# Three 256-column products per row tile in place of one of 512 and one of 256, with the operand rows packed in halves

## The chip, the cores and the metric

The kernel runs on one core of one Trainium2 chip. The core has five engines that work side by side: TensorE (PE in the profile; its weight loads are listed apart as PEld), VectorE (DVE), ScalarE (ACT), GpSimd (POOL) and SyncE (SP, which here issues DMAs). A product on TensorE has a stationary side of 128x128 numbers, loaded before it, and a moving side of up to 512 columns that is read from SBUF and added into a PSUM bank of 512 float32 columns. The metric is the time of one execution on the device in microseconds; 1596.77 us before the change (median of three runs, 1596.67 to 1596.89).

## What is computed

One decoder layer over 256 tokens and 16 meta tokens, model width 2048, all in float32:

```python
def hybrid_mixer(xn, w_in, ...):
    proj = xn @ w_in                       # 2048 x 13336
    ...                                    # forgetting attention (8 heads), gated linear attention (4 heads)
    y = sigmoid(gate_fox) * (o_fox @ w_o_fox) + sigmoid(gate_gla) * (o_gla @ w_o_gla)
    return y @ w_out

h = h + hybrid_mixer(rmsnorm(h, norm_mix_g), ...)
h = h + square(relu(rmsnorm(h, norm_mlp_g) @ w_ff1)) @ w_ff2     # 2048 -> 8192 -> 2048
return rmsnorm(h, final_norm_g)[:, 16:]
```

Nearly all of the work is in matrices times 256 or 272 tokens: `w_in`, `w_o_fox`, `w_o_gla`, `w_out`, `w_ff1`, `w_ff2`.

## The kernel before

Activations lie transposed, channels on the 128 partitions and tokens along the row. To reach float32 accuracy with TensorE's faster float32r type, both sides are cut in two: `hi` is the number rounded to float32r, `lo` is what is left. A product of two such numbers takes three partial products, hi by hi, hi by lo and lo by hi.

The weights come in blocks of 2048x128 (`w_all`, in the order of `stream()`), each as two halves of 8 row tiles. For each half SP loads `raw` (512 KB), ScalarE copies it to `whi` (line 120), VectorE subtracts to `wlo` (line 121). Five buffers of each kind go round.

One block is then multiplied by an *operand* of 16 row tiles (`of` has 8): `x` (the normalised input), `of` and `og` (the outputs of the two attentions), `y` (their gated sum), `x2` (the normalised residual) and `a` (the squared ReLU, one for each of four groups `g` of 2048 channels). The profile leaves numbers out of names, so its `x` stands for `x` and `x2`.

`gemm2` (line 139) does it: for each row tile `k`, `mac2` issues two products. Line 136 multiplies `whi` by 512 columns, the 256 columns of hi and the 256 of lo side by side, into a whole PSUM bank. Line 137 multiplies `wlo` by the 256 columns of hi into the bank's first half. The bank's halves must be added at the end: `total` (line 165) and `add_residual` (line 856) copy the second half to `evb` on ScalarE (lines 168 and 858) and add on VectorE (lines 171 and 860).

`operand` (line 218) lays a row tile out in 544 elements, of which 512 are used, from element 16: hi's 256 columns, then lo's 256. So each row tile starts 2176 bytes behind the one before.

`x` has a layout of its own (272 columns, with the meta tokens) and is used by `gemm_all` (lines 153 to 155, three products of 272 columns) and by `gemm2`. The first seven blocks have their own products (lines 345 and 350). In the last four blocks of `w_ff2` all `lo` products come first (line 912), and then the `hi` products by token halves (line 928), where one product reads 128 columns of hi and 128 columns of lo: two runs with 128 columns between them.

TensorE's order of products is that of the source, moved by a scheduler that interleaves the next block's first row tiles with the last ones of the block before where weights are ready early.

Of the kernel before, what the change touches and what calls it, by code (L numbers as in the profile page):

```python
# [7 lines left out]
F32 = mybir.dt.float32  # L8
F32R = mybir.dt.float32r
# [3 lines left out]
ALU = mybir.AluOpType  # L13
# [52 lines left out]
def trunk(ctx: ExitStack, tc: tile.TileContext, hT, w_small, w_all, consts, w_alpha2, out):  # L66
# [3 lines left out]
    def nm(s):  # L70
        serial[0] += 1
        return f"{s}_{serial[0]}"
# [11 lines left out]
    def bank(pool, s):  # L84
        return pool.tile([P, 512], F32, tag="bank", name=nm(s))
# [49 lines left out]
    def mac2(ps, hi, lo, x, first, last):  # L135
        nc.tensor.matmul(ps, hi, x, start=first, stop=False)  # L136
        nc.tensor.matmul(ps[:, 0:NT], lo, x[:, 0, :], start=False, stop=last)  # L137

    def gemm2(w, x, k0=0, nk=KT):

        ps = bank(pg, "ps")
        for k in range(nk):
            hi, lo = w(k0 + k)
            mac2(ps, hi, lo, x[:, k], k == 0, k == nk - 1)
        issued()
        return ps
# [18 lines left out]
    def total(ps, t=None):  # L165

        b = tmp.tile([P, NT], F32, tag="evb", name=nm("evb"))
        nc.scalar.copy(b, ps[:, NT:512])  # L168
        if t is None:
            t = tmp.tile([P, NT], F32, tag="evt", name=nm("evt"), bufs=4)  # L170
        nc.vector.tensor_tensor(t, ps[:, 0:NT], b, op=ALU.add)  # L171
        return t

    def split_to(dst_hi, dst_lo, src):
        nc.scalar.copy(dst_hi, src)
        nc.vector.tensor_tensor(dst_lo, src, dst_hi.bitcast(F32), op=ALU.subtract)
# [40 lines left out]

    def operand(pool, name, nk=KT, at=0, **kw):


        row = 2 * NT + 32
        t = pool.tile([P, at + nk * row], F32R, name=nm(name), **kw)
        t = t[:, at:].rearrange("p (k r) -> p k r", r=row)
        return t[:, :, 16 : 16 + 2 * NT].rearrange("p k (o t) -> p k o t", t=NT)


    h = keep.tile([P, KT, NA + 3], F32, name="h")
# [26 lines left out]
    def gain(i, k):  # L254
        return h[:, k, NA + i : NA + i + 1]
# [201 lines left out]

    def og_tile():
        if not og_box:
            og_box.append(operand(keep, "og", tag="s2"))  # L460
        return og_box[0]

    def gla_gates(ts):
# [30 lines left out]
    def gla_head(hd, sg, ready=None):  # L494
# [129 lines left out]
        def scale():  # L624
            for i in range(4):
                j = 4 * hd + i
                nc.vector.scalar_tensor_tensor(oT[:, i, :], oT[:, i, :], ggn[:, j : j + 1], rg, op0=ALU.mult,
                                               op1=ALU.mult)
                nc.vector.tensor_tensor(oT[:, i, :], oT[:, i, :], st["sg"][:, i, :], op=ALU.mult)
                split_to(og_tile()[:, j, 0, :], og_tile()[:, j, 1, :], oT[:, i, :])  # L630

        later(2, outputs)
        later(3, sums)
# [48 lines left out]
    cum.close()  # L682
    branches = ExitStack()
    late = branches.enter_context(tc.tile_pool(name="late", bufs=1, reuse_waits="tile"))
    of = operand(late, "of", FOX_H, 32)
    negc = late.tile([P, FOX_H, NA], F32, name="negc")
    nc.gpsimd.dma_start(negc.rearrange("p h t -> p (h t)"), fdram.to_broadcast([P, FOX_H * NA]))
    fox = ExitStack()
# [16 lines left out]
    def fox_head(hd):  # L705
# [71 lines left out]
        def out_v():  # L777
            po = bank(px, "pof")
            three(po[:, 0:NT], va, pa, True, False)
            nc.tensor.matmul(po[:, P:NT], vb, pT, start=False, stop=True)  # L780
            nc.scalar.copy(of[:, hd, 0, :], po[:, 0:NT])
            nc.vector.tensor_tensor(of[:, hd, 1, :], po[:, 0:NT], of[:, hd, 0, :].bitcast(F32),
                                    op=ALU.subtract)
            nc.scalar.copy(og4[:, four], corners(po[:, 0:NT]))

        def out_corners():
# [9 lines left out]
        def fill_corners(pu, vz, pz):  # L796
            nc.tensor.matmul(pu[:, 2 * P : 3 * P], vz, pz, start=True, stop=True)
            nc.vector.tensor_tensor(og4, og4, pu[:, 2 * P : 3 * P].rearrange("p (h c q) -> p h c q", c=2, q=NM),
                                    op=ALU.add)
            hi, lo = (of[:, hd - 3 : hd + 1, o, :].rearrange("p h (c q) -> p h c q", q=P)[:, :, :, P - NM :]  # L800
                      for o in range(2))
            split_to(hi, lo, og4)

        later(1, turn_v)
        later(2, turn_p)
# [20 lines left out]
    for j0 in range(0, KT, 2):  # L826
        gates = ahead if j0 == 0 else [gate() for _ in range(4)]
        w = next_weights()
        for j in range(2):
            t = total(gemm2(w, of, k0=8 * j, nk=8))  # L830
            nc.vector.tensor_tensor(gates[2 * j], gates[2 * j], t, op=ALU.mult)
        for j in range(2):
            t = total(gemm2(next_weights(), og))
            nc.vector.tensor_tensor(t, gates[2 * j + 1], t, op=ALU.mult)
            nc.vector.tensor_tensor(yf[:, j0 + j, :], gates[2 * j], t, op=ALU.add)
    y = operand(keep, "y", tag="s1")
    for j in range(KT):
        split_to(y[:, j, 0, :], y[:, j, 1, :], yf[:, j, :])
    mix.close()
    branches.close()  # L840
    gat = ctx.enter_context(tc.tile_pool(name="gat", bufs=2, reuse_waits="tile"))
# [1 line left out]


    ht = h[:, :, NM:NA]
    x2 = operand(keep, "x2", tag="s2")

    def square_sum(j, acc):
        if j == 0:
# [4 lines left out]
            nc.gpsimd.tensor_tensor(acc, acc, sq, op=ALU.add)  # L854

    def add_residual(j, ps):
        b = tmp.tile([P, NT], F32, tag="evb", name=nm("evb"))
        nc.scalar.copy(b, ps[:, NT:512])
        nc.vector.tensor_tensor(ht[:, j, :], ps[:, 0:NT], ht[:, j, :], op=ALU.add)
        nc.vector.tensor_tensor(ht[:, j, :], ht[:, j, :], b, op=ALU.add)  # L860

    acc2 = gat.tile([P, NT], F32, tag="acc", name="acc2", bufs=1)
    for j in range(KT):
        add_residual(j, gemm2(next_weights(), y))
        nc.scalar.activation(x2[:, j, 0, :], ht[:, j, :], AF.Identity, scale=gain(1, j))
        nc.vector.scalar_tensor_tensor(x2[:, j, 1, :], ht[:, j, :], gain(1, j),
                                       x2[:, j, 0, :].bitcast(F32), op0=ALU.mult, op1=ALU.subtract)
        square_sum(j, acc2)
    r2b = keep.tile([P, NT], F32, tag="rb", name="r2b")

# [4 lines left out]


    def relu2(a, f, ps):
        t = total(ps)
        nc.vector.scalar_tensor_tensor(t, t, 0.0, r2b, op0=ALU.max, op1=ALU.mult)
        s = gat.tile([P, NT], F32, tag="asq", name=nm("asq"))  # L880
        nc.vector.tensor_tensor(s, t, t, op=ALU.mult)
        split_to(a[:, f, 0, :], a[:, f, 1, :], s)

    acc = gat.tile([P, NT], F32, tag="acc", name="acc3", bufs=1)
    for g in range(NG):
        a = operand(keep, "a", tag="s1")
        held = []
        for f in range(KT):
            ps = gemm2(next_weights(), x2)
            if g == 0 and f == 0:  # L890
                held.append(ps)
                continue
            if g == 0 and f == 1:
                relu2(a, 0, held.pop())
            relu2(a, f, ps)
        last = g == NG - 1
        for j in range(KT - NL if last else KT):
            add_residual(j, gemm2(next_weights(), a))
            if last:
                square_sum(j, acc)  # L900
                nc.scalar.activation(ht[:, j, :], ht[:, j, :], AF.Identity, scale=gain(2, j))
                if j == 0:
                    tc.keep_in_program_order(nc.scalar.preload_act_table_set("natural_log_exp_and_others"))


    whi = keep.tile([P, NL, KT, P], F32R, tag="s2", name="whi_last")
    ends = []
    for n in range(NL):
        j, ps = KT - NL + n, bank(pg if n < 3 else px, "ps")
        w = next_weights(whi[:, n])  # L910
        for k in range(KT):
            nc.tensor.matmul(ps[:, 0:NT], w(k)[1], a[:, k, 0, :], start=(k == 0), stop=(k == KT - 1))  # L912
        nc.vector.tensor_tensor(ht[:, j, :], ps[:, 0:NT], ht[:, j, :], op=ALU.add)
        ends.append((j, w, ps))

    def half(t0, between, within=None):


        tok = slice(t0, t0 + P)
        sqs = []  # L920
        for n, (j, w, ps) in enumerate(ends):
            for k in range(KT):
                if within and n == NL - 1 and k == 4:
                    ahead = within()
                elif not (within and n == NL - 1 and k > 4):
                    ahead = None
                with tc.issue_after(ahead) if ahead else nullcontext():
                    nc.tensor.matmul(ps[:, NT:], w(k)[0], a[:, k, :, tok], start=(k == 0), stop=(k == KT - 1))  # L928
            between[n]()
            for t in (ps[:, NT : NT + P], ps[:, NT + P :]):  # L930
                nc.vector.tensor_tensor(ht[:, j, tok], t, ht[:, j, tok], op=ALU.add)
            sq = gat.tile([P, P], F32, tag="sq", name=nm("sq"), bufs=4)
            nc.scalar.activation(sq, ht[:, j, tok], AF.Square)
            nc.scalar.activation(ht[:, j, tok], ht[:, j, tok], AF.Identity, scale=gain(2, j))
            if n < NL - 2:
                nc.gpsimd.tensor_tensor(acc[:, tok], acc[:, tok], sq, op=ALU.add)
            else:
                sqs.append(sq)
        return sqs
# [119 lines left out]
```

## Time and profile before

| what | value |
|---|---|
| median of three runs | 1596.77 us |
| profiled execution, span | 1595.0 us |
| PE, 9812 products | busy 99% of the span |
| PEld, 9812 weight loads | 90% |
| VectorE | 66% |
| ScalarE | 50% |
| DMA engines, mean | about half busy, 184 GB/s |
| granted TensorE clock | 1.00 of full speed from 0 to 1400 us, 0.99 after |

How to read it: a product's duration in the profile is from its start to the end of its passage through the array, and products overlap. A product of 512 columns is listed with 393 ns and one of 256 columns with 281 ns, but the next one starts earlier than that. What a product costs when the array is never idle is the time from its start to the next start. The chain view gives that: its pieces are times between starts, and their sum is the span.

### The profile page before, as it was taken

Reading aid. Unit: us, or ns where it says so; the run is one execution under the profiler, and the core shown is the slowest. Engines: PE = TensorE matmul, PEld = TensorE weight load, DVE = VectorE, ACT = ScalarE, POOL = GpSimd, SP = SyncE. Lnnn points to the kernel's source line nnn. Section 1 sums busy time; section 2 is a strip of 40 time slices with the busy share of each in tenths; the row PEclk is TensorE's granted clock in tenths of the full one; section 3 lists DMA queues with packets and bytes.
Section 4 is the critical chain, followed back from the end, with each engine's and each line's share of the span. In section 5 each row is a group of like instructions: output and inputs, shape, how many; then the busy total and the mean of one; then the engine's idle time right before and its main releaser. Section 6 shows DMA issues by size and latency. Waiting matters only on the chain.

```text
span 1595.0 us, 25427 instructions
## 1 busy us (share of the span) xinstructions
PE 1585.0 (99%) x9812; PEld 1428.8 (90%) x9812; DVE 1060.4 (66%) x1659; ACT 790.8 (50%) x1271; POOL 125.2 (8%) x213
## 2 busy tenths in 40 slices
PE   9999999999999999999999999999999999999997
PEld 8999999999998888888888888888888888888887
DVE  7897757676655555555777776567655776567655
ACT  6665444454455444444555544444444444444563
POOL 6011000011100000000011000000000000000022
PEclk9999999999999999999999999999999999999999
DMA  9444545454445555555555555555555555555552
GB/s 323 156 164 155 180 157 183 167 188 164 159 167 181 191 186 189 189 191 187 186 195 186 188 193 187 188 191 190 187 190 190 186 189 193 186 188 193 186 183 97
DMA packets 86602, 293.09 MB, mean 184 GB/s; under 512 B 9112, under 2 KB 16800, under 8 KB 86352
## 3 DMA queue, kind: packets, MB, share of 16 engines
q1 hardware_dynamic: 85872, 289.62, 53.8%
q8 instruction: 77, 1.26, 0.3%
q0 software_dynamic: 176, 1.12, 0.2%
q10 hardware_dynamic: 432, 0.72, 0.1%
q14 instruction: 45, 0.37, 0.1%
HBM read 289.32 MB, written 2.11 MB: 183 GB/s over the span
## 4 chain that ended last, share of the span: by engine, by line
PE 99%; DMA 0%; issue 0%; POOL 0%; ACT 0%; DVE 0%; SPq 0%; POOLq 0%; ACTq 0%
PE ps L136 51%; PE ps L137 27%; PE psa L155 5%; PE psa L154 5%; PE psa L153 5%; PE ps L345 1%; PE ps L350 1%; PE ps L928 1%; PE pa L548 1%; PE ps L912 0%; DMA raw<-w_all_dram 0%; PE po L611 0%; POOL o L976 0%; PE po L188 0%; PE ps L348 0%
## 5 line engine op out<-in xcount | busy, mean ns | idle before, releaser
L121 DVE TENSOR_TENSOR wlo<-raw,whi 128x1024 fp32r<-128x1024 f32 x522 | 641.0, 1228 | 452.8 <-ACT whi L120 449.4
L120 ACT CAST whi<-raw 128x1024 fp32r<-128x1024 f32 x522 | 548.1, 1050 | 660.0 <-PE ps L136 493.1
L136 PE MATMUL ps<-x,whi 128*128 128x512 f32 x1952 | 683.8, 393 | 0.0
L137 PE MATMUL ps<-x,wlo 128*128 128x256 f32 x1952 | 548.5, 281 | 0.0
L136 PEld LDWEIGHTS ps<-x,whi 128*128 128x128 f32 x1952 | 366.1, 188 | 80.4
L137 PEld LDWEIGHTS ps<-x,wlo 128*128 128x128 f32 x1952 | 368.3, 189 | 0.1
L136 PE MATMUL ps<-a,whi 128*128 128x512 f32 x960 | 334.3, 392 | 0.0
L137 PE MATMUL ps<-a,wlo 128*128 128x256 f32 x960 | 269.1, 281 | 0.0
L136 PEld LDWEIGHTS ps<-a,whi 128*128 128x128 f32 x960 | 179.8, 188 | 39.9
L137 PEld LDWEIGHTS ps<-a,wlo 128*128 128x128 f32 x960 | 181.1, 189 | 0.3
L153 PE MATMUL psa<-x,whi 128*128 128x272 f32 x624 | 181.2, 290 | 0.0
L155 PE MATMUL psa<-x,whi 128*128 128x272 f32 x624 | 181.1, 290 | 0.0
L154 PE MATMUL psa<-x,wlo 128*128 128x272 f32 x624 | 179.4, 288 | 0.0
L153 PEld LDWEIGHTS psa<-x,whi 128*128 128x128 f32 x624 | 118.1, 189 | 0.4
L154 PEld LDWEIGHTS psa<-x,wlo 128*128 128x128 f32 x624 | 117.4, 188 | 0.0
L155 PEld LDWEIGHTS psa<-x,whi 128*128 128x128 f32 x624 | 117.2, 188 | 0.0
L136 PE MATMUL ps<-og,whi 128*128 128x512 f32 x256 | 89.6, 392 | 0.0
L136 PE MATMUL ps<-y,whi 128*128 128x512 f32 x256 | 89.1, 392 | 0.0
L854 POOL TENSOR_TENSOR acc<-acc,hsq 128x256 f32<-128x256 f32 x26 | 28.5, 1097 | 769.2 <-ACT hsq L853 769.2
L137 PE MATMUL ps<-og,wlo 128*128 128x256 f32 x256 | 71.9, 281 | 0.0
L137 PE MATMUL ps<-y,wlo 128*128 128x256 f32 x256 | 71.8, 281 | 0.0
L171 DVE TENSOR_TENSOR evt<-ps,evb 128x256 f32<-128x256 f32 x158 | 65.9, 418 | 0.5 <-ACT evb L168 0.5
(301 smaller groups left out, 1437.0 us busy)
## 6 DMA issues: line engine op xcount, KB each, us to landing
raw<-w_all_dram SPq DMA_DIRECT2D x537, 512.0 KB, 3.6
raw<-w_all_dram SPq DMA_DIRECT2D x8, 384.0 KB, 6.6
h<-hT_dram SPq DMA_DIRECT2D x8, 275.0 KB, 6.7
negc<-fdram POOLq DMA_DIRECT2D x1, 1088.0 KB, 8.0
out_dram<-o SPq DMA_DIRECT2D x2, 512.0 KB, 2.7
raw<-w_all_dram SPq DMA_DIRECT2D x2, 256.0 KB, 3.9
room<-w_small_dram SPq DMA_DIRECT2D x1, 320.0 KB, 7.4
out_dram<-o ACTq DMA_DIRECT2D x1, 320.0 KB, 3.1
```

The lines of the kernel that those rows point to most:

```text
L120: nc.scalar.copy(hi[:, k, :], r)
L121: nc.vector.tensor_tensor(lo[:, k, :], r, hi[:, k, :].bitcast(F32), op=ALU.subtract)
L136: nc.tensor.matmul(ps, hi, x, start=first, stop=False)
L137: nc.tensor.matmul(ps[:, 0:NT], lo, x[:, 0, :], start=False, stop=last)
L153: nc.tensor.matmul(ps[:, 0:NA], hi, x_hi[:, k], start=(k == 0), stop=False)
L154: nc.tensor.matmul(ps[:, 0:NA], lo, x_hi[:, k], start=False, stop=(k == KT - 1))
L155: nc.tensor.matmul(ps[:, X_LO], hi, x_lo[:, k], start=False, stop=(k == KT - 1), skip_group_check=True)
L171: nc.vector.tensor_tensor(t, ps[:, 0:NT], b, op=ALU.add)
L345: nc.tensor.matmul(ps, hi, x[:, k], start=st, stop=False)
L350: nc.tensor.matmul(ps[:, 0:NT], lo, x[:, k, 0], start=False, stop=sp)
L548: nc.tensor.matmul(dst, k[:, a], q[:, a, :], start=(a == 0), stop=(a == 1))
L854: nc.gpsimd.tensor_tensor(acc, acc, sq, op=ALU.add)
```

## The change

A new function `gemm3` replaces `gemm2` wherever the operand is `of`, `og`, `y`, `x2` or `a`. It issues three products of 256 columns for each row tile: `whi` by hi, `whi` by lo and `wlo` by hi, all three into the first half of the bank. Products with `x` keep `gemm2` and `gemm_all`. As the bank then holds the finished sum, the copy to `evb` and the addition behind it go, in all five uses.

The operands are laid out anew. A row tile takes 512 elements with no gap between tiles: 128 columns of hi, 128 of lo, 128 of hi, 128 of lo. A product of 256 columns therefore reads two separate runs of 128. What used to be one run in each row tile of VectorE's and ScalarE's writes becomes two (`pair` shapes the source alike). The parameter `at` says how many elements lie ahead of the first row tile, and differs: 64 for `og` and `x2`, 96 for `of` and `y`, 96, 64, 80, 64 for the four `a`. The kept weights of the last four blocks start 16 elements later, and there the `hi` products by token halves now read 256 columns in one run.

```diff
+    def gemm3(w, x, k0=0, nk=KT):
+        ps = bank(pg, "ps")[:, 0:NT]
+        for k in range(nk):
+            hi, lo = w(k0 + k)
+            nc.tensor.matmul(ps, hi, x[:, k, 0], start=(k == 0), stop=False)
+            nc.tensor.matmul(ps, hi, x[:, k, 1], start=False, stop=False)
+            nc.tensor.matmul(ps, lo, x[:, k, 0], start=False, stop=(k == nk - 1))
+        issued()
+        return ps
...
     def operand(pool, name, nk=KT, at=0, **kw):
-        row = 2 * NT + 32
-        t = pool.tile([P, at + nk * row], F32R, name=nm(name), **kw)
-        t = t[:, at:].rearrange("p (k r) -> p k r", r=row)
-        return t[:, :, 16 : 16 + 2 * NT].rearrange("p k (o t) -> p k o t", t=NT)
+        t = pool.tile([P, nk * (2 * NT + 32)], F32R, name=nm(name), **kw)
+        return t[:, at : at + nk * 2 * NT].rearrange("p (k a o t) -> p k o a t", a=2, o=2, t=P)
+    def pair(ap):
+        return ap.rearrange("p (a t) -> p a t", t=P)
...
         for j in range(2):
-            t = total(gemm2(w, of, k0=8 * j, nk=8))
+            t = gemm3(w, of, k0=8 * j, nk=8)
             nc.vector.tensor_tensor(gates[2 * j], gates[2 * j], t, op=ALU.mult)
...
     def add_residual(j, ps):
-        b = tmp.tile([P, NT], F32, tag="evb", name=nm("evb"))
-        nc.scalar.copy(b, ps[:, NT:512])
-        nc.vector.tensor_tensor(ht[:, j, :], ps[:, 0:NT], ht[:, j, :], op=ALU.add)
-        nc.vector.tensor_tensor(ht[:, j, :], ht[:, j, :], b, op=ALU.add)
+        nc.vector.tensor_tensor(ht[:, j, :], ps, ht[:, j, :], op=ALU.add)
...
     def relu2(a, f, ps):
-        t = total(ps)
-        nc.vector.scalar_tensor_tensor(t, t, 0.0, r2b, op0=ALU.max, op1=ALU.mult)
+        t = tmp.tile([P, NT], F32, tag="evt", name=nm("evt"), bufs=4)
+        nc.vector.scalar_tensor_tensor(t, ps, 0.0, r2b, op0=ALU.max, op1=ALU.mult)
         s = gat.tile([P, NT], F32, tag="asq", name=nm("asq"))
         nc.vector.tensor_tensor(s, t, t, op=ALU.mult)
-        split_to(a[:, f, 0, :], a[:, f, 1, :], s)
+        split_to(a[:, f, 0], a[:, f, 1], pair(s))
...
-        a = operand(keep, "a", tag="s1")
+        a = operand(keep, "a", at=(96, 64, 80, 64)[g], tag="s1")
...
-    whi = keep.tile([P, NL, KT, P], F32R, tag="s2", name="whi_last")
+    whi = keep.tile([P, 16 + NL * KT * P], F32R, tag="s2", name="whi_last")[:, 16:].rearrange(
+        "p (n k m) -> p n k m", k=KT, m=P)
...
-                    nc.tensor.matmul(ps[:, NT:], w(k)[0], a[:, k, :, tok], start=(k == 0), stop=(k == KT - 1))
+                    nc.tensor.matmul(ps[:, NT:], w(k)[0], a[:, k, :, t0 // P], start=(k == 0), stop=(k == KT - 1))
```

On TensorE, in the middle of a block of `w_ff1` (the names are the PSUM tile, then the operand `x2` and the weight half), three row tiles before:

```order
L136 MATMUL ps_11435<-x_1469_8671,whi_11424 128x512
L137 MATMUL ps_11435<-x_1469_8671,wlo_11425 128x256
L136 MATMUL ps_11435<-x_1469_8671,whi_11430 128x512
L137 MATMUL ps_11435<-x_1469_8671,wlo_11431 128x256
L136 MATMUL ps_11435<-x_1469_8671,whi_11430 128x512
L137 MATMUL ps_11435<-x_1469_8671,wlo_11431 128x256
```

and now two row tiles:

```order
L144 MATMUL ps_12785<-x_1421_8943,whi_12774 128x256
L145 MATMUL ps_12785<-x_1421_8943,whi_12774 128x256
L146 MATMUL ps_12785<-x_1421_8943,wlo_12775 128x256
L144 MATMUL ps_12785<-x_1421_8943,whi_12774 128x256
L145 MATMUL ps_12785<-x_1421_8943,whi_12774 128x256
L146 MATMUL ps_12785<-x_1421_8943,wlo_12775 128x256
```

A row tile has one product more, with the same weights as the one before it; the columns are 768 as before.

On VectorE in the same stage (`evt` is the sum of the two halves, `asq` the square, `a` the operand written; line 121 makes weights), before:

```order
L176 TENSOR_TENSOR a_11206<-asq_11635,a_11206 128x256
L121 TENSOR_TENSOR wlo_11803<-raw_11801,whi_11802 128x1024
L171 TENSOR_TENSOR evt_11686<-ps_11651,evb_11684 128x256
L879 TENSOR_SCALAR evt_11686<-evt_11686,r2b 128x256
L881 TENSOR_TENSOR asq_11689<-evt_11686 128x256
L121 TENSOR_TENSOR wlo_11809<-raw_11807,whi_11808 128x1024
```

and now:

```order
L121 TENSOR_TENSOR wlo_12641<-raw_12639,whi_12640 128x1024
L187 TENSOR_TENSOR a_12102<-asq_12501,a_12102 128x2x128
L121 TENSOR_TENSOR wlo_12647<-raw_12645,whi_12646 128x1024
L883 TENSOR_SCALAR evt_12566<-ps_12517,r2b 128x256
L885 TENSOR_TENSOR asq_12568<-evt_12566 128x256
L121 TENSOR_TENSOR wlo_12708<-raw_12706,whi_12707 128x1024
```

The addition of line 171 is gone and the next step reads PSUM itself; the writes of `a` are in two runs. The rest stands as it stood.

More of the change, by code (lines that the diff above doesn't have):

```diff
@@ L459, in og_tile @@
         if not og_box:
-            og_box.append(operand(keep, "og", tag="s2"))
+            og_box.append(operand(keep, "og", at=64, tag="s2"))
         return og_box[0]
@@ L629, in scale @@
                 nc.vector.tensor_tensor(oT[:, i, :], oT[:, i, :], st["sg"][:, i, :], op=ALU.mult)
-                split_to(og_tile()[:, j, 0, :], og_tile()[:, j, 1, :], oT[:, i, :])
+                split_to(og_tile()[:, j, 0], og_tile()[:, j, 1], pair(oT[:, i, :]))
         later(2, outputs)
@@ L684, in trunk @@
     late = branches.enter_context(tc.tile_pool(name="late", bufs=1, reuse_waits="tile"))
-    of = operand(late, "of", FOX_H, 32)
+    of = operand(late, "of", FOX_H, 96)
     negc = late.tile([P, FOX_H, NA], F32, name="negc")
@@ L780, in out_v @@
             nc.tensor.matmul(po[:, P:NT], vb, pT, start=False, stop=True)
-            nc.scalar.copy(of[:, hd, 0, :], po[:, 0:NT])
-            nc.vector.tensor_tensor(of[:, hd, 1, :], po[:, 0:NT], of[:, hd, 0, :].bitcast(F32),
-                                    op=ALU.subtract)
+            split_to(of[:, hd, 0], of[:, hd, 1], pair(po[:, 0:NT]))
             nc.scalar.copy(og4[:, four], corners(po[:, 0:NT]))
@@ L799, in fill_corners @@
                                     op=ALU.add)
-            hi, lo = (of[:, hd - 3 : hd + 1, o, :].rearrange("p h (c q) -> p h c q", q=P)[:, :, :, P - NM :]
-                      for o in range(2))
-            split_to(hi, lo, og4)
+            split_to(*(of[:, hd - 3 : hd + 1, o, :, P - NM :] for o in range(2)), og4)
         later(1, turn_v)
@@ L829, in trunk @@
         for j in range(2):
-            t = total(gemm2(w, of, k0=8 * j, nk=8))
+            t = gemm3(w, of, k0=8 * j, nk=8)
             nc.vector.tensor_tensor(gates[2 * j], gates[2 * j], t, op=ALU.mult)
         for j in range(2):
-            t = total(gemm2(next_weights(), og))
-            nc.vector.tensor_tensor(t, gates[2 * j + 1], t, op=ALU.mult)
+            t = tmp.tile([P, NT], F32, tag="evt", name=nm("evt"), bufs=4)
+            nc.vector.tensor_tensor(t, gates[2 * j + 1], gemm3(next_weights(), og), op=ALU.mult)
             nc.vector.tensor_tensor(yf[:, j0 + j, :], gates[2 * j], t, op=ALU.add)
-    y = operand(keep, "y", tag="s1")
+    y = operand(keep, "y", at=96, tag="s1")
     for j in range(KT):
-        split_to(y[:, j, 0, :], y[:, j, 1, :], yf[:, j, :])
+        split_to(y[:, j, 0], y[:, j, 1], pair(yf[:, j, :]))
     mix.close()
@@ L845, in trunk @@
     ht = h[:, :, NM:NA]
-    x2 = operand(keep, "x2", tag="s2")
+    x2 = operand(keep, "x2", at=64, tag="s2")
     def square_sum(j, acc):
@@ L856, in add_residual @@
     def add_residual(j, ps):
-        b = tmp.tile([P, NT], F32, tag="evb", name=nm("evb"))
-        nc.scalar.copy(b, ps[:, NT:512])
-        nc.vector.tensor_tensor(ht[:, j, :], ps[:, 0:NT], ht[:, j, :], op=ALU.add)
-        nc.vector.tensor_tensor(ht[:, j, :], ht[:, j, :], b, op=ALU.add)
+        nc.vector.tensor_tensor(ht[:, j, :], ps, ht[:, j, :], op=ALU.add)
     acc2 = gat.tile([P, NT], F32, tag="acc", name="acc2", bufs=1)
     for j in range(KT):
[L864 to L867, printed above, removed]
+        add_residual(j, gemm3(next_weights(), y))
+        nc.scalar.activation(x2[:, j, 0], pair(ht[:, j, :]), AF.Identity, scale=gain(1, j))
+        nc.vector.scalar_tensor_tensor(x2[:, j, 1], pair(ht[:, j, :]), gain(1, j),
+                                       x2[:, j, 0].bitcast(F32), op0=ALU.mult, op1=ALU.subtract)
         square_sum(j, acc2)
@@ L877, in relu2 @@
     def relu2(a, f, ps):
-        t = total(ps)
-        nc.vector.scalar_tensor_tensor(t, t, 0.0, r2b, op0=ALU.max, op1=ALU.mult)
+        t = tmp.tile([P, NT], F32, tag="evt", name=nm("evt"), bufs=4)
+        nc.vector.scalar_tensor_tensor(t, ps, 0.0, r2b, op0=ALU.max, op1=ALU.mult)
         s = gat.tile([P, NT], F32, tag="asq", name=nm("asq"))
         nc.vector.tensor_tensor(s, t, t, op=ALU.mult)
-        split_to(a[:, f, 0, :], a[:, f, 1, :], s)
+        split_to(a[:, f, 0], a[:, f, 1], pair(s))
     acc = gat.tile([P, NT], F32, tag="acc", name="acc3", bufs=1)
     for g in range(NG):
-        a = operand(keep, "a", tag="s1")
+        a = operand(keep, "a", at=(96, 64, 80, 64)[g], tag="s1")
         held = []
         for f in range(KT):
-            ps = gemm2(next_weights(), x2)
+            ps = gemm3(next_weights(), x2)
             if g == 0 and f == 0:
@@ L897, in trunk @@
         for j in range(KT - NL if last else KT):
-            add_residual(j, gemm2(next_weights(), a))
+            add_residual(j, gemm3(next_weights(), a))
             if last:
@@ L911, in trunk @@
         for k in range(KT):
-            nc.tensor.matmul(ps[:, 0:NT], w(k)[1], a[:, k, 0, :], start=(k == 0), stop=(k == KT - 1))
+            nc.tensor.matmul(ps[:, 0:NT], w(k)[1], a[:, k, 0], start=(k == 0), stop=(k == KT - 1))
         nc.vector.tensor_tensor(ht[:, j, :], ps[:, 0:NT], ht[:, j, :], op=ALU.add)
```

## The prediction

> **What bounds the kernel now.** I read the page first, then the waits of TensorE, then the chain of waits.
>
> ```profile
> span 1595.0 us, 25427 instructions
> PE 1585.0 (99%) x9812; PEld 1428.8 (90%) x9812; DVE 1060.4 (66%) x1659; ACT 790.8 (50%) x1271; POOL 125.2 (8%) x213
> PE 99%; DMA 0%; issue 0%; POOL 0%; ACT 0%; DVE 0%; SPq 0%; POOLq 0%; ACTq 0%
> PE ps L136 51%; PE ps L137 27%; PE psa L155 5%; PE psa L154 5%; PE psa L153 5%; PE ps L345 1%; PE ps L350 1%; PE ps L928 1%; PE pa L548 1%; PE ps L912 0%; DMA raw<-w_all_dram 0%; PE po L611 0%; POOL o L976 0%; PE po L188 0%; PE ps L348 0%
> ```
>
> The chain is TensorE from end to end, and 78% of it are the two lines of `mac2`. A busy row alone would not prove that TensorE is the limit; the list of its waits does, because it is empty between the first microseconds and the last:
>
> ```profile
> PE warm L311 <- DVE ones L195: 1.3, 1, 1.3
> PE pn L952 <- ACT sq L933: 0.7, 1, 0.7
> PE ps L345 <- ACT whi L280: 0.4, 1, 0.4
> ```
>
> 2.4 us in all, none of it in the stages that change. So the time is the number of products times the gap between two starts, and only that gap counts here.
>
> The gap of a row tile comes from the chain between two like points of the feed-forward stage, one for each group `g`:
>
> ```profile
> 969.30 0.46 PE ps L136 x2
> 1147.64 0.46 PE ps L136 x2
> 1325.99 0.46 PE ps L136 x2
> 1504.34 0.46 PE ps L136 x2
> ```
>
> From 969.30 to 1504.34 are 535.04 us for three groups of 32 blocks of 16 row tiles, 1536 row tiles: **348.3 ns for a row tile of 512 + 256 columns.** The split between the two shows where the same form stands several times in a row, in the first blocks:
>
> ```profile
> 21.19 0.92 PE ps L345 x4
> 22.11 0.47 PE ps L350 x4
> ```
>
> 0.92 / 4 = 230 ns for 512 columns, 0.47 / 4 = 117.5 ns for 256; with 348.3 known, 231 and 117.3. Twice the columns cost 1.97 times the time, so cutting 512 into two products loses only 2 x 117.3 - 231 = 3.6 ns, if all products of 256 cost alike.
>
> **The change part by part.**
>
> *The products.* By the program, `gemm3` serves 2624 row tiles: `of` 128, `og` 256, `y` 256, `x2` 1024, `a` 3 x 256 + 192. What one of its products costs is not in these rows, for its read is in two runs of 128 columns. But the last four blocks before the change have just that form, also with a weight load for each product, and beside them stands the form in one run:
>
> ```profile
> 1562.51 5.68 PE ps L912 x48
> 1571.96 7.47 PE ps L928 x64
> L928 PE MATMUL ps<-a,whi_last x128: 277/279/365, 1568.0 to 1585.4; 128*128 128x256 f32 x128
> L912 PE MATMUL ps<-a,wlo x64: 276/280/283, 1562.3 to 1571.7; 128*128 128x256 f32 x64
> L153 PE MATMUL psa<-x,whi x624: 282/288/401, 49.9 to 466.6; 128*128 128x272 f32 x156
> L154 PE MATMUL psa<-x,wlo x624: 282/287/291, 50.1 to 466.7; 128*128 128x272 f32 x156
> ```
>
> One run: 5.68 / 48 = 118.3 ns. Two runs: 7.47 / 64 = **116.7 ns.** Two runs are no dearer, if anything cheaper. Three times 116.7 are 350.1, against 348.3: 1.8 ns more for a row tile, 4.7 us in all.
>
> That is a mean over places. A place is the distance, modulo 512 bytes, from the start of the moving read to the start of the weights loaded meanwhile, by the addresses of the built programs. Before, row tiles are 2176 bytes apart and the place changes with each; after, they are 2048 apart, and an operand keeps one place for all its products. So I sorted the starts of the groups above by place. Two runs (L928, 121 gaps): 115.4 ns at 64, 118.4 at 192, 115.6 at 320, 118.0 at 448. Products of 272 columns (L153 to L155): 123.4 at 64, 125.3 at 192, 123.9 at 320, 125.6 at 448, 128.7 at 256. The order of the places is the same in both. For 256 columns take 16 columns off the latter: (231 - 117.3) / 256 = 0.444 ns a column, 7.1 ns.
>
> After, by the addresses: place 320 for `of`, `og`, `x2` and the second and fourth `a` (1856 row tiles), 192 for `y` and the first `a` (512), 256 for the third `a` (256).
>
> - Place 320: 115.6 from the same form, 123.9 - 7.1 = 116.8 from the wider one. I take the middle, 116.2, because the same form changed place with every product and the wider one kept it for two at a time. 3 x 116.2 - 348.3 = +0.3 ns, x 1856 = **+0.6 us** (from -2.8 to +3.9).
> - Place 192: 118.4 and 118.2; 118.4, the same form. +6.9 ns x 512 = **+3.5 us.**
> - Place 256: no row has two runs there. Bounds: one run of 256 (L912 sorted alike) 117.2 ns, 272 columns 128.7 - 7.1 = 121.6. Between: in the first blocks (L350), where the place stays for four products, those behind the first one of a run at 0 or 256 took 119.75. I take that, since it is the only row with a place that stays: 359.25 - 348.3 = +10.9 ns x 256 = **+2.8 us** (+0.8 to +4.2).
>
> Sum **+6.9 us.**
>
> The Trainium skill ("TensorE: Matmul & The Clock Gate", Part 2, Step-by-step) says that TensorE has two independent read ports and that loading the next weights takes no read bandwidth from the running product. By that the place could not matter, and the sum would be the 4.7 us of the mean. The sorted gaps differ by 3 ns between places, so the trace speaks against it.
>
> *The evictions.* Gone are 172 copies on ScalarE and as many additions on VectorE (16 + 16 + 64 by `total`, 16 + 60 by `add_residual`):
>
> ```profile
> L168 ACT COPY evb<-ps x160: 358/366/401, 41.8 to 1496.5; 128x256 f32<-128x256 f32 x160
> L858 ACT COPY evb<-ps x76: 354/367/368, 792.3 to 1564.4; 128x256 f32<-128x256 f32 x76
> L171 DVE TENSOR_TENSOR evt<-ps,evb x158: 411/418/425, 43.1 to 1497.8; 128x256 f32<-128x256 f32 x158
> L860 DVE TENSOR_TENSOR h<-h,evb x76: 420/426/430, 795.4 to 1566.3; 128x256 f32<-128x256 f32 x76
> ```
>
> 172 x 0.366 = 63 us of ScalarE, 96 x 0.418 + 76 x 0.426 = 72.5 us of VectorE. I cost them at nothing: TensorE's work covers them, as its list of waits shows. Without that cover each eviction would have cost its 0.8 us. Earlier free banks gain nothing either, since no product waits for one; and writes in two runs, were each to cost VectorE and ScalarE a tenth more, stay below what is removed.
>
> *Supply of weights.* The weight blocks, their loads and cuts stay as they are; a block takes 5.57 us of TensorE (16 x 348.3 ns) against
>
> ```profile
> L121 DVE TENSOR_TENSOR wlo<-raw,whi 128x1024 fp32r<-128x1024 f32 x522 | 641.0, 1228 | 452.8 <-ACT whi L120 449.4
> ```
>
> 2 x 1.23 us of VectorE. The 2624 added weight loads repeat the one before them, of `whi`; at a product for each load L928 shows no more than the gap above, so they are in its price.
>
> *The end.* The last four blocks swap one and two runs for 192 products: 118.3 to 116.2 for 64 and 116.7 to about 116.8 for 128, -0.1 us; nothing.
>
> **The rivals.**
>
> *Faster: a place that stays lets reads and loads fall into step.* Two runs at place 64 took 115.4 on the mean, but once the sequence of L928 had settled 114.4 again and again. Below 116.1 a product gains on before. Were 114.4 the price at place 320, that is -5.1 ns x 1856 = -9.5, with +3.5 and +2.8 -3.2 us, 1593.6; if at all places, -5.1 x 2624 = -13.4 us, 1583.4. For it: each product in L928 followed one at another place, so no row shows two runs at a place that stays. Against it: the first blocks, in one run, kept a place for four products and grew dearer there (119.75), not cheaper.
>
> *No change: places even out.* If the settled price is 116.1 everywhere, three products are 348.3 and the time stays at 1596.8. For it: 7.47 / 64 is only 0.6 ns away. Against it: the 3 ns between places.
>
> *Much slower: the settled price is that of the dear place.* All at 119.75: +10.9 x 2624 = +28.7 us, 1625.5. For it: the L350 rows. Against it: these are in one run, and L928 shows no such value on the mean.
>
> *The copies were what mattered.* Then some TensorE wait would end at `evb`; none does. No chance given.
>
> **How the numbers follow.** The sum is for the profiled execution, 1595.0 us of span; the median of the runs lies 1.8 us above it, so 1596.8 + 6.9 = 1603.7. Chances: forecast (1599 to 1611) 0.54, faster 0.26, no change 0.12, much slower 0.08. About 0.2%, 3.2 us, is what can be told from no change; of the forecast's own range its lowest microsecond falls within that, which adds 0.02 to no change. So faster 0.26, same 0.14, slower 0.60. The range takes in the nearer half of the faster cases and the first third of the way to the dear one: 1587 to 1615.
>
> **What would show it.** TensorE still at 99% with no wait in the changed stages; 9812 + 2624 = 12436 products; in the chain, row tiles of `x2` and of the second and fourth `a` near 349 ns, of `y` and the first `a` near 355, of the third `a` near 359. `evb` left only with `x`. It is wrong if `x2`, most of the row tiles, comes out below 345 or above 352 ns, or if all operands cost the same whatever their place, or if TensorE now waits for something.

## The result and the profile after

The change takes 1591.07 us (median of six runs, 1589.22 to 1592.89) against 1596.83 us for the kernel before: ratio 0.9964, 95% interval 0.9952 to 0.9975. It is faster by 0.36%, where 1603.7 us was forecast.

The page of the changed kernel's profile, the lines that answer to those shown of before:

```profile
span 1590.7 us, 30310 instructions
PE 1580.0 (99%) x12436; PEld 1533.7 (96%) x12436; DVE 1003.6 (63%) x1487; ACT 747.1 (47%) x1099; POOL 126.9 (8%) x213
...
PE ps L145 19%; PE ps L144 19%; PE ps L146 19%; PE ps L136 13%; PE ps L137 7%; PE psa L166 5%; PE psa L165 5%; PE psa L164 5%; PE ps L356 1%; PE ps L933 1%; PE ps L361 1%; PE pa L559 1%; PE ps L917 0%; DMA raw<-w_all_dram 0%; PE po L622 0%
```

TensorE is still the whole chain, with 12436 products in place of 9812. VectorE and ScalarE have lost 57 and 44 us of work, and no part of the chain got shorter by it. So the gap between two starts decides, as forecast.

The gap can be read from a view by stretches of time, which counts the products in each: a stretch of 70 us also holds the 2.4 products or so that began before it (279 ns each), so the gap is 70 us / (count - 2.4). The columns are the stretch, its length, busy time and count of TensorE, the granted clock, DMA share and GB/s. The changed kernel, in stretches that each hold one operand: `y`, `x2`, first `a`, `x2`, second `a`, third `a`:

```profile
790.00:860.00 70.00, 70.00 (x597) 1.00 0.58 187
890.00:960.00 70.00, 70.00 (x597) 1.00 0.58 186
970.00:1040.00 70.00, 70.00 (x596) 1.00 0.57 185
1060.00:1130.00 70.00, 70.00 (x620) 1.00 0.61 194
1150.00:1220.00 70.00, 70.00 (x620) 1.00 0.59 194
...
1320.00:1390.00 70.00, 70.00 (x586) 1.00 0.57 183
```

597 products are a gap of 117.7 ns, 620 are 113.3 and 586 are 119.9. `y` and the first `a` (place 192) have 117.7, the third `a` (place 256) has 119.9, the second `a` (place 320) has 113.3. But `x2`, all of it at place 320, has both: 117.7 in the first group and 113.3 in the second. The starts themselves, sorted by operand, show that these are two settled states and no mixture: 113, 113, 114 ns over and over in one, 118, 117, 118 in the other. I call them the short and the long gap.

What happened to `x2` near 889 us stands in the timeline (start, duration, engine, line, operation; in brackets the idle time before):

```profile
888.00 0.28 PE L146 MATMUL ps<-x,wlo 128*128 128x256 f32 x1
...
888.05 0.42 DVE L227 SCALAR_TENSOR_TENSOR r2b<-acc,r2b 128x256 f32<-128x256 f32 x1
888.11 0.28 PE L144 MATMUL ps<-x,whi 128*128 128x256 f32 x1
...
888.23 0.28 PE L145 MATMUL ps<-x,whi 128*128 128x256 f32 x1
...
888.34 0.28 PE L146 MATMUL ps<-x,wlo 128*128 128x256 f32 x1
888.51 1.09 DVE L883 SCALAR_TENSOR_TENSOR evt<-ps,r2b 128x256 f32<-128x256 f32 x3
...
889.04 0.19 PEld L144 LDWEIGHTS ps<-x,whi 128*128 128x128 f32 x1 [0.63 <-issue]
889.08 0.35 PE L144 MATMUL ps<-x,whi 128*128 128x256 f32 x1 [0.46 <-DVE evt L883]
889.15 0.19 PEld L145 LDWEIGHTS ps<-x,whi 128*128 128x128 f32 x1
889.27 0.28 PE L145 MATMUL ps<-x,whi 128*128 128x256 f32 x1
889.27 0.19 PEld L146 LDWEIGHTS ps<-x,wlo 128*128 128x128 f32 x1
889.39 0.28 PE L146 MATMUL ps<-x,wlo 128*128 128x256 f32 x1
```

TensorE pauses at the fourth block of `w_ff1` for a PSUM bank (0.46 us idle, 0.74 us from start to start): line 883 now reads PSUM itself and needs the norm `r2b`, which line 227 finishes only here, so three banks stay held until the norm is there; before, `total` emptied them without it. Ahead of the pause the starts are 0.113 us apart, behind it 0.118, for the 13 blocks left in the stage.

### The profile page after: what moved, and what is told of

It is laid out like the page before. It is cut to its first block, busy times and chain, and to the rows that moved or that the text cites. A ratio compares the mean times of both kernels' runs of the same rounds, so it can differ in the third digit from the quotient of the medians.

```text
span 1590.7 us, 30310 instructions
## 1 busy us (share of the span) xinstructions
PE 1580.0 (99%) x12436; PEld 1533.7 (96%) x12436; DVE 1003.6 (63%) x1487; ACT 747.1 (47%) x1099; POOL 126.9 (8%) x213
## 4 chain that ended last, share of the span: by engine, by line
PE 98%; DMA 0%; DVE 0%; issue 0%; ACT 0%; POOL 0%; SPq 0%; POOLq 0%; ACTq 0%
PE ps L145 19%; PE ps L144 19%; PE ps L146 19%; PE ps L136 13%; PE ps L137 7%; PE psa L166 5%; PE psa L165 5%; PE psa L164 5%; PE ps L356 1%; PE ps L933 1%; PE ps L361 1%; PE pa L559 1%; PE ps L917 0%; DMA raw<-w_all_dram 0%; PE po L622 0%
## 5 line engine op out<-in xcount | busy, mean ns | idle before, releaser
L136 PE MATMUL ps<-x,whi 128*128 128x512 f32 x928 | 326.9, 394 | 0.0
L144 PE MATMUL ps<-x,whi 128*128 128x256 f32 x1024 | 284.0, 277 | 0.5 <-DVE evt L883 0.5
L145 PE MATMUL ps<-x,whi 128*128 128x256 f32 x1024 | 284.0, 277 | 0.0
L145 PE MATMUL ps<-a,whi 128*128 128x256 f32 x960 | 268.0, 279 | 0.0
L144 PE MATMUL ps<-a,whi 128*128 128x256 f32 x960 | 267.8, 279 | 0.0
L136 PEld LDWEIGHTS ps<-x,whi 128*128 128x128 f32 x928 | 174.1, 188 | 37.0
L144 PEld LDWEIGHTS ps<-x,whi 128*128 128x128 f32 x1024 | 193.2, 189 | 0.6 <-issue 0.6
L145 PEld LDWEIGHTS ps<-x,whi 128*128 128x128 f32 x1024 | 192.3, 188 | 0.0
L144 PEld LDWEIGHTS ps<-a,whi 128*128 128x128 f32 x960 | 181.5, 189 | 0.0
L145 PEld LDWEIGHTS ps<-a,whi 128*128 128x128 f32 x960 | 181.4, 189 | 0.0
L164 PEld LDWEIGHTS psa<-x,whi 128*128 128x128 f32 x624 | 118.2, 189 | 0.4
```

Of the source, the lines that this page charges most:

```text
L144: nc.tensor.matmul(ps, hi, x[:, k, 0], start=(k == 0), stop=False)
L145: nc.tensor.matmul(ps, hi, x[:, k, 1], start=False, stop=False)
L164: nc.tensor.matmul(ps[:, 0:NA], hi, x_hi[:, k], start=(k == 0), stop=False)
```

## The experiments

Places are as in the prediction: bytes, modulo 512, from the start of the moving read to the start of the weights loaded meanwhile. Gaps are means over all products of an operand.

**p1: other places.**

```diff
-    y = operand(keep, "y", at=96, tag="s1")
+    y = operand(keep, "y", at=16, tag="s1")
-        a = operand(keep, "a", at=(96, 64, 80, 64)[g], tag="s1")
+        a = operand(keep, "a", at=(112, 48, 32, 0)[g], tag="s1")
```

> One look at the places that the change does not use: y at 0, the four a at 128, 384, 448 and 64, the others at 320 as they were. Theory (the place alone sets the gap, and places 256 bytes apart are alike): 0 like 256 with 120 ns a product, 448 like 192 with 117.7, 64 like 320 with 113.4 or, where it settles in the slower of its two states, 117.8; 128 and 384 alike, near 119 by the rows of 272 columns before (126 less 7). Rival (the gap hangs on the operand or the stage, not on the place): y and the first a stay at 117.7, the third a at 120, the others at 113.4. Time 1586 to 1594 us by either; the gaps by operand tell.

1597.02 us in one run. The stretches of `y` (place 0) and the four `a` (128, 384, 448, 64):

```profile
790.00:860.00 70.00, 70.00 (x586) 1.00 0.54 183
...
970.00:1040.00 70.00, 70.00 (x592) 1.00 0.55 186
...
1150.00:1220.00 70.00, 70.00 (x592) 1.00 0.54 184
...
1320.00:1390.00 70.00, 70.00 (x597) 1.00 0.56 187
...
1500.00:1560.00 60.00, 60.00 (x532) 1.00 0.59 197
```

119.9, 118.7, 118.7, 117.7 and (60 / 529.6) 113.3 ns: every one as expected from its place, and in the first three `a` something else than in the change. The operand and its stage don't matter; places 256 apart are alike. The time is above the range expected: `y` and the first two `a` met dearer places and only the third `a` a cheaper one, which by these gaps adds 4.9 us to the change's profiled run (1592.38 us): the range was added up wrongly, not the gaps.

**p2: everything at place 320.**

```diff
-    y = operand(keep, "y", at=96, tag="s1")
+    y = operand(keep, "y", at=64, tag="s1")
-        a = operand(keep, "a", at=(96, 64, 80, 64)[g], tag="s1")
+        a = operand(keep, "a", at=(64, 64, 64, 64)[g], tag="s1")
```

> y and the first and third a move to place 320. Theory (place): their products go from 117.7 and 120 ns to 113.4, or to 117.8 where they settle in the slower state: 1579 us with all in the fast state, 1589 us with all three in the slow one. Rival (by operand or stage): no change, 1591 us.

1581.53, 1581.59 and 1581.73 us in three runs, 1607.93 in one more. The mean granted clock is 0.998 in all four, so the long run is the kernel's own doing. The profile is of that run. Its stretches of `y`, `x2` and the second `a`:

```profile
790.00:860.00 70.00, 70.00 (x597) 1.00 0.56 187
...
1060.00:1130.00 70.00, 70.00 (x596) 1.00 0.55 188
1150.00:1220.00 70.00, 70.00 (x597) 1.00 0.56 187
```

The long gap, from `y` to the end; the expectation had let only the three moved operands go long (1589 us). (1607.93 - 1581.6) us over the 2240 row tiles from `y` on are 11.8 ns each, close to 3 x (117.8 - 113.3) = 13.5; the three short runs left no profile. So the same program, same addresses, has two settled gaps 4.4 ns apart, and once in the long one it stayed there for 800 us.

**p3: one run in place of two.**

```diff
-        ...rearrange("p (k a o t) -> p k o a t", a=2, o=2, t=P)
+        ...rearrange("p (k o a t) -> p k o a t", a=2, o=2, t=P)
```

(on p2)

> As p2, but a row tile is 256 columns of hi and then 256 of lo, so each product reads one run at the same place 320. Theory (the place alone, and that it stays): 113.4 or 117.8 ns, time as p2. Rival (the two runs are needed): 118 to 120 ns a product for 2624 row tiles, 1597 to 1612 us.

1608.16 us in one run. The view of two stretches with `of` and `og`, then of one with `x2`:

```profile
573.00:586.00 13.00, 13.00 (x117) 1.00 0.58 196
612.00:625.00 13.00, 13.00 (x113) 1.00 0.57 192
1060.00:1130.00 70.00, 70.00 (x597) 1.00 0.56 188
```

13 us / 114.6 is 113.4 ns, 13 / 110.6 is 117.5: both gaps are there with one run too, and `x2` sat in the long one, as in p2's long run. The two separate runs are not what gives the short gap. Whether one run reaches it as often was not tried.

**p4 and p10: two products in rows that keep their place.** The kernel before with

```diff
-        t = pool.tile([P, at + nk * row], F32R, name=nm(name), **kw)
-        t = t[:, at:].rearrange("p (k r) -> p k r", r=row)
-        return t[:, :, 16 : 16 + 2 * NT].rearrange("p k (o t) -> p k o t", t=NT)
+        t = pool.tile([P, nk * row], F32R, name=nm(name), **kw)
+        return t[:, at : at + nk * 2 * NT].rearrange("p (k o t) -> p k o t", o=2, t=NT)
```

and `at` such that all lie at 320 (p4), or at eight places (p10).

> The kernel before with one thing of the change: row tiles 512 elements apart, so that each operand keeps place 320. Products of 512 and 256 columns, copies and additions as before. Theory (a place that stays is all that gains): the row tile falls from 348.3 to about 340 ns, 1575 us with what the third product saves. Rival (three equal products are needed for reads and loads to fall in step): 346 to 350 ns, 1591 to 1601 us. Rival (the copies to evb on ScalarE were the cost): no gain here, 1597 us.

> Products of 512 and 256 columns as before, in rows that keep their place, each operand at another one: og 448, y 0, x2 256, the four a 64, 128, 192, 384, of 320. Theory (three equal products with one load each are needed for the fast state): no row tile under 343 ns at any place; those at 0, 128, 256, 384 near the sorted gaps of before, 347.6, 348.9, 346.2, 350.1 ns. Rival (512 and 256 have a fast state too, and p4 only met the slow one): 338 to 342 ns at 64 or another place.

p4: 1610.00 us (1609.82 to 1610.07), ratio 1.0083, interval 1.0066 to 1.0100. p10: 1606.09 us in one run. One stretch of `x2` before, in p4 and in p10 (place 256):

```profile
890.00:960.00 70.00, 70.00 (x404) 1.00 0.56 190
```

```profile
890.00:960.00 70.00, 70.00 (x398) 1.00 0.55 185
```

```profile
890.00:960.00 70.00, 70.00 (x399) 1.00 0.55 187
```

By the starts in the profiled run, a row tile takes 235.0 + 118.3 = 353.3 ns in p4 (352.3 in `of`); in p10 between 351.0 (128 and 384) and 353.3 (64, 192, 448). None of these eight places gives 512 + 256 columns a short gap, and a place that stays is dearer for them than one that moves (348.3). So the layout alone gains nothing; products of equal length are needed as well. The values expected for 0, 128 and 256 (346 to 349) missed, by the same mistake as in the prediction: they were sorted from products whose neighbours lay elsewhere.

These two runs settle one more rival. All the experiments move the operand and none the weights, which for nearly all products start at the same address modulo 512; the operand's own address might decide, and not its distance to the weights. But the kept weights of the last four blocks start 64 bytes earlier in the kernel before, and so in p4 and p10. There the products of 256 columns of line 927 read the last `a`, which by its own address would stand at 320 in p4 and at 384 in p10, but at 256 and 320 by the distance to the weights. The chain in p4, then in p10:

```profile
1584.73 7.68 PE ps L927 x64
```

```profile
1581.64 7.26 PE ps L927 x64
```

7.68 / 64 is 120.0 ns, the gap of place 256; 7.26 / 64 is 113.4, the short gap of 320, where place 384 had 118.7 in p1. So it is the distance that decides. And as these products have one load of other weights each, the short gap doesn't need the same weights twice in a row.

**p6 and p9: the evictions put back.** In both hi by lo adds into the bank's second half. In p6 the copy and an addition into PSUM follow in `gemm3` and the rest is as in the change; in p9 `total`, `add_residual` and `relu2` are those of before.

```diff
+            nc.tensor.matmul(ps[:, NT:], hi, x[:, k, 1], start=False, stop=(k == nk - 1), skip_group_check=True)
...
-        nc.vector.scalar_tensor_tensor(t, ps, 0.0, r2b, op0=ALU.max, op1=ALU.mult)
+        t = total(ps)
+        nc.vector.scalar_tensor_tensor(t, t, 0.0, r2b, op0=ALU.max, op1=ALU.mult)
```

> The change with the evictions as they were: the hi by lo product adds into the second half of the bank, and a copy to evb on ScalarE and an addition on VectorE follow each block. Layout and places as in the change. Theory (the gain lies in the gap between products, not in the evictions): 1589 to 1593 us as the change. Rival (the copies and additions, or all three products adding into one half, made the gain): 1596 us or more.

> The change with the evictions word for word as before: hi by lo adds into the second half of the bank, then the copy to evb, the addition, and only then the step that needs the norm. Places and layout as in the change. In p6 the banks stayed held until the norm was known, here they don't. Theory (the gain is the gap between products at place 320): 1588 to 1593 us, no TensorE wait of over 1 us in w_ff1. Rival (the removed evictions, or adding into one half, are the gain): 1596 us or more with the gaps as before.

p6: 1597.69 us (median of ten runs, 1596.12 to 1609.47), the rival's number. But its list of waits has a new first row, which p9's has not, and the stretch behind that wait a lower granted clock:

```profile
PE ps L145 <- DVE evt L887: 4.3, 1, 4.3
...
890.00:960.00 70.00, 67.04 (x556) 0.98 0.53 171
```

p6 holds three banks until the norm is known, as the change does, and adds work ahead of it on VectorE: 4.3 us of pause in place of 0.5, another 1.1 us near the end, and 1.4 us by the clock (70 x 0.02) are 6.3 of the 6.6 us that its median lies above the change's. These are read from its longest run, 1609.47 us, the only one with a profile, which had the long gap in `x2` and the second `a` from the pause until the third `a` besides; that the other nine runs pause alike is likely, not shown. p9, whose banks are freed as before, takes 1589.63 us (1589.12 to 1590.91), ratio 0.9954, interval 0.9938 to 0.9969: no slower than the change, with all evictions back, though it too pauses 1.1 us near the end. So neither the evictions nor the half bank made the gain.

**p5, p11, p7: ways back to the short gap.** p5 and p11 are the change with

```diff
-        a = operand(keep, "a", at=(96, 64, 80, 64)[g], tag="s1")
+        a = operand(keep, "a", at=(96, 64, 64, 64)[g], tag="s1")     # p5: places 192, 320, 320, 320
+        a = operand(keep, "a", at=(80, 64, 64, 64)[g], tag="s1")     # p11: places 256, 320, 320, 320
```

and p7 is p2 with the first row tile of `og`, `y`, `x2` and each `a` at place 256 and 112 unused elements between it and the others.

```diff
+        first, rest = rows(at, 1), rows(at + 2 * NT + 112, nk - 1)
```

> The change with the third a moved from place 256 to 320; the first a stays at 192. Theory (place 320 has a fast state, 113.4 ns a product, and a slow one, 117.8; a wait of TensorE can throw it into the slow one, where it stays while every product has place 320; products at another place lead back to the fast one): the wait behind the first block of w_ff1 does its harm to x2, the first a at 192 ends it, all groups behind are fast: the third a saves 256 x 3 x 6.6 ns, 5.1 us, 1584 to 1587 us in every run. Rival (the state is drawn anew by chance at each operand): runs spread up to 20 us, some over 1595.

> As p5, with the first a at 256 in place of 192. One run of p5 took 1608 us. Theory (place 192 leads back to the fast state only at times, place 256 always): 256 x 3 x 2.2 ns = 1.7 us more than p5's good runs, 1586 to 1589 us in every run. Rival (chance at every operand): again some run over 1595 us.

> As p2 (all at place 320), but the first row tile of og, y, x2 and each a lies at place 256. Theory (products at another place lead back to the fast state): every block starts with three products of 120 ns and is fast behind them: 156 row tiles at 360 ns, 2340 at 340.2, of as before: 1596.8 + 1.8 - 19.0 = 1579.6 us, in every run within 1 us. Rival (three products don't suffice, or the state is drawn by chance): runs between 1580 and 1608 us as p2's, with whole stages at 117.8.

p5: 1584.36, 1584.53, 1586.88 and 1608.38 us. The expectation of one good time in every run fell. The run of 1608.38 us left no profile; its time is about what the long gap gives in `x2` and all `a` at 320, so by its time a whole operand at 192 leads back to the short gap in most runs, not all. p11: 1585.89 to 1589.39 us in five runs, none long, which fits the sharper statement about 256 but doesn't prove it in five runs. p7: 1581.83 us (1581.16 to 1582.60), ratio 0.9908, interval 0.9891 to 0.9925, and every stretch of the feed-forward stages is alike:

```profile
612.00:625.00 13.00, 13.00 (x114) 1.00 0.62 190
790.00:860.00 70.00, 70.00 (x618) 1.00 0.59 194
1060.00:1130.00 70.00, 70.00 (x617) 1.00 0.60 194
1320.00:1390.00 70.00, 70.00 (x618) 1.00 0.59 192
```

618 are 113.7 ns. It missed its forecast by 2 us; `of`, which was left as it was, and with it some blocks of `og`, still take the long gap in places (first row, 116.5 ns). p7 beats both kernels, and no run of it was long.

**p8: places between.**

> Places between those used so far: y at 288, the four a at 352, 304, 224 and 336, the others as in the change. Theory (reads and loads meet in parts of 64 bytes or more): 304 and 336 like 320 with 113.4 or 117.8 ns, 288 and 352 between that and the neighbours (120 and 119), 224 near 118 to 120. Rival (only the start on a multiple of 64 bytes helps): all of them 118 to 122 ns. Time 1586 to 1600 us.

1595.87 us in one run. `y` at 288 and `a` at 352, 304, 224, 336: 118.3, 117.3, 119.2, 116.7 and 119.3 ns. 304 and 336, only 16 bytes to either side of 320, have no short gap; of the 13 places tried, only 64 and 320 showed it. So the theory fell and the rival was nearer, though 352 and 224 lie below its 118 to 122 ns. Places other than 192, 256 and 320 stood in one run only, and one run can't show whether they too settle in two ways.

The same profile has the pause at the fourth block of `w_ff1` (0.5 us in its list of waits), and yet the first `x2`, at 320 as in the change, stays short behind it:

```profile
890.00:960.00 70.00, 70.00 (x620) 1.00 0.59 193
```

So the pause doesn't tip the gap every time.

**p12: no pause.** The first three blocks of `w_ff1` are copied out of PSUM at once:

```diff
+            if g == 0 and f < 3:
+                copied.append(tmp.tile([P, NT], F32, tag="evt", name=nm("evt"), bufs=4))
+                nc.scalar.copy(copied[-1], ps)
+                ps = copied[-1]
```

> The change, but the first three blocks of w_ff1 are copied out of PSUM by ScalarE at once, so that no bank waits for the norm. Theory (the wait of 0.7 us at the fourth block throws x2 into the slow state in about half of the runs, for 13 blocks x 48 products x 4.4 ns = 2.7 us): all runs at 1589 to 1590 us, none at 1592. Rival (the spread of the change has another cause): runs between 1589 and 1593 us as before.

1588.72 us (1588.46 to 1589.08), and the first `x2` is short:

```profile
890.00:960.00 70.00, 70.00 (x619) 1.00 0.57 192
```

The 3.7 us of spread of the change have become 0.6. p9, which has no pause there either, is short in the same stretch too (x620). So it is the pause that threw `x2` into the long gap in the change's profiled run (1592.38 us). The runs near 1589 us probably had the pause and stayed short behind it, as p8 did; they left no profile.

## Why the prediction was wrong

*What bounds it* was right: TensorE's gap alone. *Evictions at nothing* was right to about 1 us: p9, with all of them, takes 1589.63 us, p12, with three copies, 1588.72. But one side of them was overlooked. "Earlier free banks gain nothing" held, while three banks are now freed later, behind the norm, and that pause, 0.74 us from start to start, costs another 13 x 48 x 4.4 ns = 2.7 us where the gap behind it is long.

*Place 192*: 118.4 forecast, 117.7 found. *Place 256*: 119.75 forecast, 119.9 found. The latter came from the only rows of before in which a place stayed for several products.

**The step that failed is the term for place 320**, 1856 row tiles: 116.2 ns a product, +0.6 us, with bounds of -2.8 to +3.9. Found are 113.3 and 117.7. In the profiled run `of` and `og` (384 row tiles, half in each state, 346.7 ns) give -0.6 us, `x2` (208 at 353.3, 816 at 340.0) -5.7, second and fourth `a` (448 at 340.0) -3.7: -10.0 us in place of +0.6. With +2.6 for place 192 and +3.0 for 256 the sum is -4.4 us; the spans differ by -4.3. `x2` shows it by the sign that the prediction named: below 345 or above 352 ns, and 340.0 and 353.3 came. Both the value and the bounds (115.6 to 116.8 ns a product) were built on means of products whose place changed with each one, or with every second. A mean like that is not the price of a place that stays: this settles at 113.3, below the bounds, or at 117.7, above them. A hint was on record: the same sequence of L928 that was averaged to 115.4 showed 114.4 once settled, and the rival built on that put 1593.6 us, 2.5 us from the result. It had this much right, that a place that stays can be cheaper; that its sum came so near is luck, for 114.4 is neither of the two gaps, only near the mixture of the profiled run (1856 row tiles with -10.0 us are 114.3 ns a product).

The argument against that rival, that the first blocks "grew dearer" when a place stayed, was from places 0 and 256, where it holds (119.9); it was carried over to 320, where it doesn't. Even in those blocks it held for half of the rows only: by the starts in the trace, rows of four at places 128 and 384 took 117.7 ns for the first product and 117.8 on the mean behind it, so there it didn't grow dearer.

The Trainium skill's rule on the two read ports ("TensorE: Matmul & The Clock Gate", Part 2, Step-by-step), weighed in the prediction, fits these runs no better than the rows before: with a load for each product the gap goes from 113.3 to 119.9 ns with the distance between the two reads.

What stays open: what the two reads share, why 320 settles in two ways (64 showed only the short gap, in one run), and what decides which of them a run gets. That a pause can tip the gap from short to long is shown (the change's own profile, p12); it doesn't each time (p8). That products at 256 tip it back each time is only likely (p7, p11).

## What to carry to other kernels

When TensorE never waits, its gap is worth measuring by address: three equal products at one good distance between moving read and weights took 340 ns, when they settled well, where 512 + 256 columns took 348 to 353. Price such a layout from products that stay at one distance, never from a mean over several. And mind the spread of the runs: two clusters of times can be one loop that settles in two ways, which a short pause can tip and a few products at another distance seem to undo.

## What was not expected of the hardware

- A stream of identical products (256 columns, float32r, a load of 128x128 before each) settles at 113.3 or at 117.7 ns at the same addresses, and stayed at either for hundreds of microseconds (short from 1060 to 1560 us in p5's profile, long from 790 to 1560 us in p2's; whole runs of p2 took 1581.6 or 1607.9 us).
- Shifting the moving read by 16 bytes, from 320 to 304 or 336, costs 5.9 ns a product over the short gap, 1.5 over the long one (p8).
- With products of 512 and 256 columns in turn, a fixed distance cost 351 to 353 ns at all eight places tried, a moving one 348.3.
